# Other PSUM banks for four steps of a two-layer transformer kernel, and the last columns in quarters

## The chip, the core and the metric

The kernel runs on one core of a Trainium2 chip. The core has a matrix engine (TensorE, in the profile PE, with its weight loads shown apart as PEld), a vector engine (VectorE, DVE), a scalar engine (ScalarE, ACT), a general engine (GpSimd, POOL) and SyncE (SP), which here only issues transfers. Each engine runs its own instructions in order and waits on semaphores for the others. Data lies in SBUF; TensorE writes its sums into PSUM, which the kernel uses as eight banks of 128 partitions by 512 floats.

The metric is the device time of one launch in microseconds (us). Three runs of the kernel before took 711.92, 708.44 and 712.90 us, the median is 711.92. The profiled execution took 712.76 us; its span, from the first to the last instruction, is 711.0 us.

## The reference

Sixteen learned meta tokens stand ahead of 256 tokens of width 1024, so 272 columns pass through two layers. A layer is a mixer of three kinds of heads side by side, an output projection, and a feed-forward block with a squared ReLU:

```python
h = jnp.concatenate([meta, x], axis=1)                    # [1, 272, 1024]
for l in range(DEPTH):                                    # 2 layers
    u = rmsnorm(h, norm_mix[l])
    (qa, ka, va, qi, ki, wi, qb, kb, vb, qc, kc, vc, gc) = jnp.split(u @ w_in[l], split_pts, axis=-1)
    a_out = sparse_indexer_attention(qa, ka, va, qi, ki, wi, bias_a, topk=64)   # 8 heads of 64
    b_heads = diff_attention(qb, kb, vb, bias_b, lam)     # 4 heads: softmax - lam * softmax
    b_out = rmsnorm(b_heads, diff_norm[l]) * (1.0 - lambda_init)
    ret = retention(rotary(qc), rotary(kc), vc)           # 4 heads
    c_out = jax.nn.silu(gc) * rmsnorm(ret, ret_norm[l])
    h = h + jnp.concatenate([a_out, b_out, c_out], axis=-1) @ w_out[l]
    u = rmsnorm(h, norm_ff[l])
    h = h + jnp.square(jax.nn.relu(u @ w_ff1[l])) @ w_ff2[l]
return rmsnorm(h, final_norm)[:, N_META:]                 # [1, 256, 1024]
```

In the indexer the scores `relu(qi . ki)`, weighted by `wi`, choose the 64 keys that each query of the first kind of heads may see.

## The kernel before

**Units.** All weights are cut into 206 units of 1024 rows by 128 columns, 103 for each layer: 31 for the input projections, 8 for the output projection, 64 for the feed-forward block. The activations lie transposed, features on partitions and tokens on columns. A unit (function `slot`) is 24 matmuls: each of its eight 128x128 blocks is multiplied three times, since weights and activations are each split into a high part and a remainder (`hi`/`lo`, `uh`/`ul`): hi by uh (L189), hi by ul (L190), lo by uh (L191), all into one PSUM bank. SyncE loads the units ahead, ScalarE makes `hi` (L170), VectorE or, for some units, GpSimd makes `lo` (L182).

**Events.** Everything that is not a unit's matmul (scores, softmax, transposes, norms) is put between them by hand. `place(slot, p, f)` hangs the step `f` on slot `slot + p // 6` at one of six points: "evac" and "none" ahead of its matmuls, "quarter" after 6 of them, "half" after 12, "most" after 18, "all" after 24. The table `PLACES` holds the number `p` of each step, the table `AFTER` the distance of the steps that follow a unit. The order of the calls is the order on every engine, so an instruction that waits holds up everything behind it on its engine.

**Banks.** The eight banks are two rotating pools of four. `acc_bank()` takes the next bank of the units' pool (`mm` in the profile), `att()` the next of the other pool (`att`). A bank is given to a new holder in the order of the calls, and its first writer waits until the last reader of the holder four calls back is done.

**The steps that the change touches**, all in `mixer` and `ffn_rows`:

- `e_ki` (L462): the indexer's keys leave the first unit's bank. The product with the token factor goes once into `f` (`kf`, in SBUF) and once, rounded, into `kh`; the two L471 subtract `kh` from `f`, for the upper and the lower 64 partitions. `i_head` (L575) multiplies the keys by the queries.
- `b_values` (L766) calls `meta_v`: two transposes (L645) into an `att` bank, and a ScalarE copy to SBUF (L647), the values of the meta tokens for the differential heads. Pair 1 of these heads (`b_pair`, L726) takes two `att` and two `mm` banks; the exponentials (L599) go back into one of the `att` banks of each head, and `b_keys` (L747) reads it last.
- `r_pv` (L803): the value sums of the differential heads (w = 0) and of the retention heads (w = 1), into one bank `o` (L811, L817, L820); in layer 0 the meta tokens' sums go to a second bank `om` (L822). `r_norm` squares them, sums, and has GpSimd raise to the power -0.5 (L837); `r_scale` reads `o` last on VectorE (L844) and `om` (L849). `a_pair` (L662) takes two `att` banks for the scores of two heads of the first kind, `a_keys` (L605, copied by L606) one for the transposed weights.
- `ffn_rows`: in layer 1 the second feed-forward product is made by rows, tokens on partitions: for each of two blocks of 128 tokens (t) and two halves of 512 columns (a) one `att` bank `acc[t, a]` sums over 32 units (`pairs`, L1019). The last unit is done one half of the columns after the other. `last(t)` then makes `y` (L1048), its squares on ScalarE (L1049), `yg` (L1054), the sum of squares (L1056), the power on GpSimd (L1058), and the output in two halves (L1059 and L1061) with a transfer each on SyncE (L1060, L1062). After the last matmul only `last(1)` is left.

Of the kernel before, what the change touches and what calls it, by code (L numbers as in the profile page):

```python
# [8 lines left out]
F = mybir.dt.float32  # L9
R = mybir.dt.float32r  # L10
AF = mybir.ActivationFunctionType
# [35 lines left out]
    "a_pair": (105, 116, 134, 148),  # L47
    "a_norm": (109, 110, 119, 127, 137, 144, 155, 156),
    "a_keys": (117, 122, 127, 138, 145, 154, 163, 168),
    "b_values": (99,),  # L50
    "b_meta": (115,),
    "e_wi2": (28,),
    "r_pv": (124, 167),
# [47 lines left out]
def block_kernel(ctx: ExitStack, tc: tile.TileContext, W, hin, cst, onehot, rbe, par, fin, dlam, out):  # L101
# [337 lines left out]
    def mixer(l):  # L439
# [21 lines left out]

        def e_ki(ps):  # L462
            bc = bcast[key]
            f = ta("kf")
            k2 = ck([128, 2, T], R, "ki")
            kh, kl = k2[:, 0], k2[:, 1]
            V.tensor_tensor(f[64:128], ps[64:128, :T], bc[64:128], OP.mult)
            V.tensor_tensor(kh[64:128], ps[64:128, :T], bc[64:128], OP.mult)
            S.activation(kh[0:64], f[64:128], AF.Copy)
            for r in (slice(64, 128), slice(0, 64)):  # L470
                V.tensor_tensor(kl[r], f[64:128], kh[64:128].bitcast(F), OP.subtract)  # L471
            st["ki"] = kh, kl
# [327 lines left out]


        def r_pv(w):
            o = att()  # L803
            om = att() if first else None
            vball = st[("vb", "vc")[w]]
            x4 = st[("wT", "sT")[w]]
# [162 lines left out]
    def ffn_rows():  # L969
# [40 lines left out]
            S.activation(hi, r[:, q0:], AF.Copy)  # L1010
            V.tensor_tensor(lo, r[:, q0:], hi.bitcast(F), OP.subtract)

        def pairs(wt, k, t, which, halves=(0, 1)):

            xh, xl = (x[:, k % 4, 16 + 128 * t:144 + 128 * t] for x in sx[k // 4])
            w = [x.rearrange("p a c -> p (a c)") for x in wt]
            for x, part in {"hi": ((xh, 0), (xl, 0)), "lo": ((xh, 1),)}[which]:
                for a in halves:
                    PE.matmul(acc[t, a], x, w[part][:, 512 * a:512 * a + 512],  # L1019
                              start=k == 0 and x is xh and part == 0, stop=k == 31 and part == 1)  # L1020

        def second(i, k):
            fire(i, "evac")
# [15 lines left out]
            pairs((hi, lo), k, 1, "lo")  # L1039
            fire(i, "all")  # L1040

        ms = small.tile([128, 4], F, name="ms", bufs=1)

        def last(t):
            y = ck([128, 1024], F, "y")
            half = [slice(0, 512), slice(512, 1024)]
            for a, c in enumerate(half):
                V.scalar_tensor_tensor(y[:, c], acc[t, a], scale["r2"][:, t:t + 1], hT[t][:, c], OP.mult, OP.add)  # L1048
                S.activation(tb("junk", (128, 512)), y[:, c], AF.Square, scale=float(D) ** -0.5,  # L1049
                             accum_out=ms[:, 2 * t + a:2 * t + a + 1])  # L1050
            g = scale["g"]
            o = ck([128, 1024], F, "fo")
            yg = tb("yg", (128, 512))
            V.tensor_tensor(yg, y[:, half[0]], g[:, half[0]], OP.mult)  # L1054
            v = small.tile([128, 1], F, name="nv")
            V.scalar_tensor_tensor(v, ms[:, 2 * t:2 * t + 1], EPS, ms[:, 2 * t + 1:2 * t + 2], OP.add, OP.add)  # L1056
            r = small.tile([128, 1], F, name="nr")
            G.tensor_tensor(r, v, nhalf[:, :1], OP.pow)  # L1058
            S.activation(o[:, half[0]], yg, AF.Copy, scale=r)  # L1059
            nc.sync.dma_start(out[128 * t:128 * t + 128, half[0]], o[:, half[0]])  # L1060
            V.scalar_tensor_tensor(o[:, half[1]], y[:, half[1]], r, g[:, half[1]], OP.mult, OP.mult)  # L1061
            nc.sync.dma_start(out[128 * t:128 * t + 128, half[1]], o[:, half[1]])  # L1062

        at(b + 1, "half", factors)
        at(b + 1, "none", gains)
# [28 lines left out]
        for n in range(4):  # L1094
            if n == 1:
                last(0)
            for halves in ((0, 1),) if n < 3 else ((0,), (1,)):
                pairs(wt[n], 28 + n, 1, "hi", halves)
                pairs(wt[n], 28 + n, 1, "lo", halves)
        last(1)  # L1100

    def ffn(l):
# [152 lines left out]
```

## Time and profile before

| what | before |
|---|---|
| runs | 711.92, 708.44, 712.90 us (median 711.92) |
| profiled execution | 712.76 us, span 711.0 us |
| TensorE busy | 697.5 us (98%), 5244 matmuls |
| VectorE busy | 452.6 us (64%) |
| ScalarE busy | 388.4 us (55%) |
| GpSimd busy | 162.6 us (23%) |
| chain that ended last | 90% TensorE, 3% VectorE |

Busy is the time in which an engine has an instruction under way, so a matmul that runs at half the clock is busy for longer and does no more. The granted clock of TensorE is shown as a share of its full speed. A wait is idle time of an engine that ended when another engine's instruction signalled. A row of the timeline gives the start of an instruction in us from the start of the span, its duration, engine, line, operation, and output <- input with shapes; behind it in brackets stand the idle time before it and what ended that.

### The profile page before, as it was taken

The page shows a single profiled execution, that of the slowest core. Times are in us where ns is not written, and L with a number is a line of the kernel's source. Part 1 is how long each engine was busy: PE and PEld are TensorE (multiplying, and loading weights), DVE is VectorE, ACT ScalarE, POOL GpSimd, SP SyncE. Part 2 cuts the span into 40 slices and gives each one's busy share as a digit, 9 for nine tenths or more (in the row PEclk, how much of TensorE's full clock was granted, in tenths as well). Part 3 has the DMA queues.
Part 4 walks back from the last instruction along what each step waited for, and adds up shares of the span by engine and source line. Part 5 has one row for each costly group of instructions (what it writes and reads, how often), then busy time and mean ns, then how long its engine had stood idle before and what let it go on. Part 6 is the DMA issues. An engine that isn't in the chain of part 4 may idle for free.

```text
span 711.0 us, 13318 instructions
## 1 busy us (share of the span) xinstructions
PE 697.5 (98%) x5244; PEld 659.3 (93%) x5244; DVE 452.6 (64%) x893; ACT 388.4 (55%) x760; POOL 162.6 (23%) x140
## 2 busy tenths in 40 slices
PE   9998989999999999999999999999999999999996
PEld 8898989889999999999999999998999999999994
DVE  6689548648676666454545887595576555555554
ACT  7557656447465555444435668655565445454443
POOL 2657544023100000000004667540420000000000
PEclk9999989999999999999999999999999999999998
DMA  9686333234465545455554434333365556655521
GB/s 329 181 242 185 107 138 119 76 133 148 149 207 177 174 169 185 156 189 167 175 182 140 163 115 150 118 119 105 133 211 205 177 191 197 199 182 181 180 87 59
DMA packets 34610, 115.57 MB, mean 163 GB/s; under 512 B 4051, under 2 KB 6388, under 8 KB 34548
## 3 DMA queue, kind: packets, MB, share of 16 engines
q1 hardware_dynamic: 31392, 110.00, 46.3%
q10 hardware_dynamic: 3156, 4.72, 2.8%
q8 instruction: 41, 0.67, 0.4%
q14 instruction: 21, 0.17, 0.1%
HBM read 113.05 MB, written 1.66 MB: 161 GB/s over the span
## 4 chain that ended last, share of the span: by engine, by line
PE 90%; DVE 3%; issue 2%; ACT 1%; POOL 1%; DMA 1%; SPq 0%; POOLq 0%; ACTq 0%
PE mm L189 23%; PE mm L191 23%; PE mm L190 23%; PE att L1019 12%; PE att L662 1%; PE att L575 1%; PE att L605 1%; PE att L817 1%; DMA h<-hin 1%; PE att L705 1%; PE att L811 1%; PE att L820 1%; PE att L711 0%; PE att L784 0%; POOL hv L837 0%
## 5 line engine op out<-in xcount | busy, mean ns | idle before, releaser
L170 ACT ACTIVATE hi<-raw 128x1024 fp32r<-128x1024 f32 (+1 forms) x205 | 215.0, 1051 | 150.3 <-issue 74.6
L189 PE MATMUL mm<-uh,hi 128*128 128x272 f32 (+1 forms) x1008 | 297.0, 295 | 0.0
L191 PE MATMUL mm<-uh,lo 128*128 128x272 f32 (+1 forms) x1008 | 289.8, 287 | 0.3 <-DVE lo L182 0.3
L190 PE MATMUL mm<-ul,hi 128*128 128x272 f32 (+1 forms) x1008 | 288.6, 286 | 0.0
L182 DVE TENSOR_TENSOR lo<-raw,hi 128x1024 fp32r<-128x1024 f32 (+1 forms) x175 | 214.5, 1245 | 21.4 <-ACT hi L170 21.4
L189 PEld LDWEIGHTS mm<-uh,hi 128*128 128x128 f32 x1008 | 191.5, 190 | 8.1 <-issue 6.1
L190 PEld LDWEIGHTS mm<-ul,hi 128*128 128x128 f32 x1008 | 191.8, 190 | 1.3
L191 PEld LDWEIGHTS mm<-uh,lo 128*128 128x128 f32 x1008 | 191.2, 190 | 1.1 <-DVE lo L182 0.8
L182 POOL TENSOR_TENSOR lo<-raw,hi 128x1024 fp32r<-128x1024 f32 x34 | 82.1, 2424 | 51.0 <-ACT hi L170 50.9
L189 PE MATMUL mm<-sh,hi 128*128 128x272 f32 x256 | 74.2, 290 | 0.0
L191 PE MATMUL mm<-sh,lo 128*128 128x272 f32 x256 | 74.1, 289 | 0.0
L190 PE MATMUL mm<-sl,hi 128*128 128x272 f32 x256 | 73.7, 288 | 0.0
L298 POOL TENSOR_TENSOR sacc<-sacc,sq 128x272 f32<-128x272 f32 (+1 forms) x24 | 23.0, 958 | 209.9 <-ACT sq L296 209.5
L1002 DVE TENSOR_TENSOR fr<-fr 128x256 f32<-128x256 f32 x32 | 13.6, 426 | 58.4 <-ACT fr L1001 58.4
L190 PEld LDWEIGHTS mm<-sl,hi 128*128 128x128 f32 x256 | 48.3, 188 | 0.0
L189 PEld LDWEIGHTS mm<-sh,hi 128*128 128x128 f32 x256 | 48.2, 188 | 0.0
L191 PEld LDWEIGHTS mm<-sh,lo 128*128 128x128 f32 x256 | 48.2, 188 | 0.0
L1058 POOL TENSOR_TENSOR nr<-nv,cs 128x1 f32<-128x1 f32 x2 | 1.1, 560 | 179.6 <-DVE nv L1056 179.6
L1019 PE MATMUL att<-hi,sh 128*128 128x512 f32 x128 | 40.2, 394 | 0.0
L1019 PE MATMUL att<-hi,sl 128*128 128x512 f32 x128 | 40.1, 393 | 0.0
L189 PE MATMUL mm<-oh,hi 128*128 128x272 f32 (+1 forms) x128 | 37.0, 289 | 0.0
L190 PE MATMUL mm<-ol,hi 128*128 128x272 f32 (+1 forms) x128 | 36.6, 286 | 0.0
(232 smaller groups left out, 932.9 us busy)
## 6 DMA issues: line engine op xcount, KB each, us to landing
raw<-w SPq DMA_DIRECT2D x203, 512.0 KB, 3.5
h<-hin SPq DMA_DIRECT2D x4, 272.0 KB, 4.2
nb<-scr ACTq DMA_DIRECT2D x4, 272.0 KB, 4.5
raw<-w ACTq DMA_DIRECT2D x4, 256.0 KB, 4.9
out_dram<-fo SPq DMA_DIRECT2D x4, 256.0 KB, 2.0
cs<-cst ACTq DMA_DIRECT2D x1, 904.0 KB
scr<-row ACTq DMA_DIRECT2D x1, 600.0 KB
nb<-scr ACTq DMA_DIRECT2D x4, 136.0 KB, 5.1
```

Source lines behind the costliest of these rows:

```text
L170: S.activation(hi[:, p], raw[:, p], AF.Copy)
L182: eng.tensor_tensor(lo[:, p], raw[:, p], hi[:, p].bitcast(F), OP.subtract)
L189: PE.matmul(ps, hi[:, k, :], xh, start=first and j == 0, stop=False)
L190: PE.matmul(ps, hi[:, k, :], xl, start=False, stop=False)
L191: PE.matmul(ps, lo[:, k, :], xh, start=False, stop=last and j == len(ks) - 1)
L298: eng.tensor_tensor(sacc[part][:, q0:], sacc[part][:, q0:], sq[:, q0:], OP.add)
L575: PE.matmul(ps[:, sl], q[:, c:c + 128], k[:, :n], start=i == 0, stop=i == 1)
L605: PE.transpose(pt[:, a * 128:a * 128 + 128], p[:, c:c + 128], ident)
L662: PE.matmul(ps[:, sl], st["qa"][r, m, c:c + 128], st["ka"][r, m, 0:n], start=True, stop=True)
L705: PE.matmul(ps[:, q0:T], vb, st["pmT"][:, q0:], start=True, stop=False)
L1002: V.tensor_tensor(r[:, q0:], r[:, q0:], r[:, q0:], OP.mult)
L1019: PE.matmul(acc[t, a], x, w[part][:, 512 * a:512 * a + 512], start=k == 0 and x is xh and part == 0, stop=k == 31 and part == 1)
```

## The change

1. `b_values` is placed at 86 in place of 99: in slot 14 after 6 matmuls ("quarter"), where it was in slot 16 after 12 ("half"). It holds for both layers.
2. `e_ki` keeps the product `f` in an `att` bank of PSUM in place of SBUF.
3. `r_pv` takes the bank `o` from the units' pool; `om` stays in the other.
4. The last two units are done for the second token block first on columns 0 to 511, then 512 to 767, then 768 to 1023. `last(1)` reads the second half by these quarters; so there are three sums of squares and two small additions. The output of both blocks is written by quarters of 256 columns: ScalarE scales columns 0 to 255 and 256 to 511, VectorE 512 to 767 and 768 to 1023, and four transfers follow, three from SyncE and one from ScalarE's queue.

```diff
-    "b_values": (99,),
+    "b_values": (86,),
...
         def e_ki(ps):
             bc = bcast[key]
-            f = ta("kf")
+            f = att()[:, :T]
...
         def r_pv(w):
-            o = att()
+            o = acc_bank()
             om = att() if first else None
...
-        def pairs(wt, k, t, which, halves=(0, 1)):
+        def pairs(wt, k, t, which, cols=(slice(0, 512), slice(512, 1024))):
...
-                for a in halves:
-                    PE.matmul(acc[t, a], x, w[part][:, 512 * a:512 * a + 512],
-                              start=k == 0 and x is xh and part == 0, stop=k == 31 and part == 1)
+                for c in cols:
+                    a, b = divmod(c.start, 512)
+                    PE.matmul(acc[t, a][:, b:b + c.stop - c.start], x, w[part][:, c],
+                              start=k == 0 and x is xh and part == 0, stop=k == 31 and part == 1 and c.stop % 512 == 0)
...
-            for a, c in enumerate(half):
-                V.scalar_tensor_tensor(y[:, c], acc[t, a], scale["r2"][:, t:t + 1], hT[t][:, c], OP.mult, OP.add)
-                S.activation(tb("junk", (128, 512)), y[:, c], AF.Square, scale=float(D) ** -0.5,
+            for a, c in enumerate([slice(0, 512), slice(512, 768), slice(768, 1024)] if t else half):
+                b, n = c.start % 512, c.stop - c.start
+                V.scalar_tensor_tensor(y[:, c], acc[t, c.start // 512][:, b:b + n], scale["r2"][:, t:t + 1],
+                                       hT[t][:, c], OP.mult, OP.add)
+                S.activation(tb("junk", (128, 512))[:, :n], y[:, c], AF.Square, scale=float(D) ** -0.5,
                              accum_out=ms[:, 2 * t + a:2 * t + a + 1])
...
-            V.scalar_tensor_tensor(v, ms[:, 2 * t:2 * t + 1], EPS, ms[:, 2 * t + 1:2 * t + 2], OP.add, OP.add)
+            if t:
+                V.scalar_tensor_tensor(ms[:, 2:3], ms[:, 2:3], EPS, ms[:, 3:4], OP.add, OP.add)
+                V.tensor_tensor(v, ms[:, 2:3], ms[:, 4:5], OP.add)
+            else:
+                V.scalar_tensor_tensor(v, ms[:, 0:1], EPS, ms[:, 1:2], OP.add, OP.add)
             r = small.tile([128, 1], F, name="nr")
             G.tensor_tensor(r, v, nhalf[:, :1], OP.pow)
-            S.activation(o[:, half[0]], yg, AF.Copy, scale=r)
-            nc.sync.dma_start(out[128 * t:128 * t + 128, half[0]], o[:, half[0]])
-            V.scalar_tensor_tensor(o[:, half[1]], y[:, half[1]], r, g[:, half[1]], OP.mult, OP.mult)
-            nc.sync.dma_start(out[128 * t:128 * t + 128, half[1]], o[:, half[1]])
+            for a in range(2):
+                c, d = slice(256 * a, 256 * a + 256), slice(512 + 256 * a, 768 + 256 * a)
+                S.activation(o[:, c], yg[:, c], AF.Copy, scale=r)
+                V.scalar_tensor_tensor(o[:, d], y[:, d], r, g[:, d], OP.mult, OP.mult)
+                (nc.scalar if a else nc.sync).dma_start(out[128 * t:128 * t + 128, c], o[:, c])
+                nc.sync.dma_start(out[128 * t:128 * t + 128, d], o[:, d])
...
+        for c in (slice(0, 512), slice(512, 768), slice(768, 1024)):
+            for n in (2, 3):
+                pairs(wt[n], 28 + n, 1, "hi", [c])
+                pairs(wt[n], 28 + n, 1, "lo", [c])
         last(1)
```

How TensorE's and VectorE's rows stand is shown at three places. A row names the line, the operation, output <- input with the tiles' numbers, and the semaphores that it waits for, by engine.

On TensorE in layer 0, before the change, the scores of pair 1 (L726) follow the units' rows, and the two transposes of `b_values` come some 50 rows behind them, inside a unit; `att` and `mm` are banks of the two pools, `kb` and `qb` keys and queries, `vbdT` the meta values.

```order
L726 MATMUL att_941<-kb_474,qb_585 128x144 [waits DVE_49]
L726 MATMUL mm_942<-kb_474,qb_585 128x144
L726 MATMUL att_943<-kb_474,qb_585 128x144 [waits Activation_49]
L726 MATMUL mm_944<-kb_474,qb_585 128x144 [waits DVE_49]
...
L191 MATMUL mm_1056<-uh_81,lo_936 128x272
L645 MATMUL att_1082<-cs_84,vbdT_121 128x128 [waits DVE_49]
L645 MATMUL att_1082<-cs_84,vbdT_121 128x128
L189 MATMUL mm_1056<-uh_81,hi_886 128x272
```

After the change, at the same place:

```order
L191 MATMUL mm_915<-uh_81,lo_834 128x272
L645 MATMUL att_922<-cs_84,vbdT_121 128x128 [waits DVE_49]
L645 MATMUL att_922<-cs_84,vbdT_121 128x128
L189 MATMUL mm_915<-uh_81,hi_740 128x272
...
L726 MATMUL att_946<-kb_474,qb_585 128x144 [waits Activation_49]
L726 MATMUL mm_947<-kb_474,qb_585 128x144
L726 MATMUL att_948<-kb_474,qb_585 128x144 [waits DVE_49]
```

The transposes now stand six unit matmuls ahead of pair 1, and the pair's two `att` banks are each one further on in the rotation: its third bank waits for VectorE where it waited for ScalarE.

The second place is the third pair of scores of the first kind of heads (`a_pair(2)`), behind the value sums of layer 0, on TensorE; `ka` and `qa` are its keys and queries. Before:

```order
L191 MATMUL mm_1421<-uh_81,lo_1300 128x272
L662 MATMUL att_1428<-ka_801,qa_1054 128x144 [waits Activation_49]
L662 MATMUL att_1429<-ka_801,qa_1054 128x144 [waits DVE_49]
L662 MATMUL att_1428<-ka_801,qa_1054 128x272
L662 MATMUL att_1429<-ka_801,qa_1054 128x272
```

After:

```order
L191 MATMUL mm_1421<-uh_81,lo_1300 128x272
L662 MATMUL att_1428<-ka_801,qa_1059 128x144
L662 MATMUL att_1429<-ka_801,qa_1059 128x144 [waits Activation_49]
L662 MATMUL att_1428<-ka_801,qa_1059 128x272
L662 MATMUL att_1429<-ka_801,qa_1059 128x272
```

The second bank waited for VectorE (L844, which reads the value sums); now it waits for ScalarE. The value sums themselves (L811 to L820) stand in the same rows as before, with `mm` in place of `att`.

The third place is the end of VectorE's program, `last(1)`; `y`, `yg`, `nv` and `fo` are the tiles of the final norm, a row with x2 stands for two. Before:

```order
L1048 SCALAR_TENSOR_TENSOR y<-att,r_6596,hT 128x512 [waits PE_49] x2
L1054 TENSOR_TENSOR yg<-y,fg 128x512 [waits DVE_49]
L1056 SCALAR_TENSOR_TENSOR nv<-ms 128x1 [waits Activation_49]
L1061 SCALAR_TENSOR_TENSOR fo<-y,nr,fg 128x512 [waits Pool_49]
```

After:

```order
L1050 SCALAR_TENSOR_TENSOR y<-att,r_6596,hT 128x512 [waits PE_49]
L1050 SCALAR_TENSOR_TENSOR y<-att,r_6596,hT 128x256 [waits PE_49]
L1050 SCALAR_TENSOR_TENSOR y<-att,r_6596,hT 128x256
L1057 TENSOR_TENSOR yg<-y,fg 128x512 [waits DVE_49]
L1060 SCALAR_TENSOR_TENSOR ms<-ms 128x1 [waits Activation_49]
L1061 TENSOR_TENSOR nv<-ms 128x1 [waits DVE_49,Activation_49]
L1069 SCALAR_TENSOR_TENSOR fo<-y,nr,fg 128x256 [waits Pool_49]
L1069 SCALAR_TENSOR_TENSOR fo<-y,nr,fg 128x256
```

The second half's `y` is two rows, of which the first carries the wait for TensorE and the second none; there is one more small sum, and the last product is two rows.

## Rows read from the trace of the kernel before

**Rows 1.** Waits of TensorE: instruction <- engine waited for: us, times, longest.

```profile
PE att L645 <- DVE bp L747: 2.3, 1, 2.3
PE att L662 <- DVE on L844: 2.0, 1, 2.0
...
PE att L575 <- DVE ki L471: 0.7, 1, 0.7
```

**Rows 2.** Table by stretches: length, PE, PEld, DVE, ACT, POOL busy, clock, DMA share, GB/s.

```profile
18.00:69.00 51.00, 50.26 (x407) 47.36 (x405) 42.03 (x151) 31.11 (x76) 33.41 (x22) 1.00 0.74 200
71.40:75.20 3.80, 3.79 (x18) 3.79 (x19) 3.65 (x10) 1.68 (x4) 3.57 (x5) 0.55 0.34 98
...
102.70:109.20 6.50, 6.50 (x28) 5.79 (x29) 5.22 (x18) 3.81 (x12) 5.39 (x6) 0.51 0.23 74
109.20:704.00 594.80, 594.65 (x4479) 562.83 (x4476) 374.50 (x653) 318.36 (x588) 102.45 (x86) 1.00 0.47 157
```

**Rows 3.** Timeline of TensorE, matmuls of units at 105 and at 109 us.

```profile
105.19 0.43 PE L189 MATMUL mm<-uh,hi 128*128 128x272 f32 x1
105.42 0.43 PE L190 MATMUL mm<-ul,hi 128*128 128x272 f32 x1
...
109.30 0.37 PE L189 MATMUL mm<-uh,hi 128*128 128x272 f32 x1
...
109.77 0.29 PE L189 MATMUL mm<-uh,hi 128*128 128x272 f32 x1
109.89 0.28 PE L190 MATMUL mm<-ul,hi 128*128 128x272 f32 x1
```

**Rows 4.** Timeline of VectorE, TensorE and ScalarE around pair 1, 56 to 73 us.

```profile
55.94 0.27 DVE L621 TENSOR_TENSOR mt<-att,nb 16x128 f32<-16x128 f32 x1
...
60.34 0.76 DVE L747 SCALAR_TENSOR_TENSOR bp<-att,bsm,bp 128x144 f32<-128x144 f32 x2
...
61.01 0.39 PE L726 MATMUL att<-kb,qb 32*128 32x144 f32 x1
...
70.39 0.97 DVE L747 SCALAR_TENSOR_TENSOR bp<-att,bsm,bp 128x144 f32<-128x144 f32 x2 [0.59 <-POOL bp L742]
...
72.48 0.37 ACT L647 ACTIVATE vm<-att 128x256 f32<-128x256 f32 x1
```

**Rows 5.** Timeline of VectorE and ScalarE around the wait at L662.

```profile
98.36 0.18 DVE L456 TENSOR_TENSOR vbdT<-mm,bf 128x32 f32<-128x32 f32 x1
...
99.56 0.47 ACT L606 ACTIVATE pT<-att 128x384 f32<-128x384 f32 x1
...
101.92 0.69 DVE L844 TENSOR_TENSOR on<-att,hv 128x512 f32<-128x512 f32 x1 [2.19 <-POOL hv L837]
...
104.09 0.31 DVE L596 CUSTOM_DVE_ANT_0 ap<-att,ap 128x144 f32<-128x144 f32 x1 [1.16 <-PE att L662]
```

**Rows 6.** Groups of VectorE by line and form: busy us, mean ns of one, idle before.

```profile
L471 DVE TENSOR_TENSOR ki<-kf,ki 64x272 fp32r<-64x272 f32 x4 | 4.5, 1123 | 0.1
L494 DVE TENSOR_TENSOR qi<-mm,qi 64x256 fp32r<-64x256 f32 x16 | 6.8, 422 | 10.6 <-ACT qi L493 10.6
...
25.23 2.60 DVE L471 TENSOR_TENSOR ki<-kf,ki 64x272 fp32r<-64x272 f32 x2
```

**Rows 7.** Timeline of all engines at the end of the program.

```profile
703.42 1.43 DVE L1048 SCALAR_TENSOR_TENSOR y<-att,r,hT 128x512 f32<-128x512 f32 x2 [1.32 <-PE att L1019]
703.68 0.39 PE L1019 MATMUL att<-lo,sh 128*128 128x512 f32 x1
704.77 0.68 DVE L1054 TENSOR_TENSOR yg<-y,fg 128x512 f32<-128x512 f32 x1
...
705.88 0.56 POOL L1058 TENSOR_TENSOR nr<-nv,cs 128x1 f32<-128x1 f32 x1 [4.56 <-DVE nv L1056]
```

**Rows 8.** Timeline of ScalarE and TensorE, two transposes of weights and the copy between.

```profile
109.36 0.49 ACT L606 ACTIVATE pT<-att 128x384 f32<-128x384 f32 x1 [0.31 <-PE att L605]
...
113.52 0.49 PE L605 MATMUL att<-cs,ap 128*128 128x128 f32 x3
```

More of the change, by code (lines that the diff above doesn't have):

```diff
@@ L1040, in second @@
             fire(i, "all")
-        ms = small.tile([128, 4], F, name="ms", bufs=1)
+        ms = small.tile([128, 6], F, name="ms", bufs=1)
         def last(t):
@@ L1096, in ffn_rows @@
                 last(0)
-            for halves in ((0, 1),) if n < 3 else ((0,), (1,)):
-                pairs(wt[n], 28 + n, 1, "hi", halves)
-                pairs(wt[n], 28 + n, 1, "lo", halves)
+            if n < 2:
+                pairs(wt[n], 28 + n, 1, "hi")
+                pairs(wt[n], 28 + n, 1, "lo")
+        for c in (slice(0, 512), slice(512, 768), slice(768, 1024)):
+            for n in (2, 3):
+                pairs(wt[n], 28 + n, 1, "hi", [c])
+                pairs(wt[n], 28 + n, 1, "lo", [c])
         last(1)
```

## The prediction

> **What bounds the kernel now.** I read the page first. TensorE is busy for nearly the whole span, and the chain that ended last is mostly its matmuls, so whatever shortens the program must shorten TensorE's row, or what follows its last matmul. The second view is the list of waits, kept to TensorE [rows 1]. It is short: 2.3 us at L645, the transposes of the first differential values; 2.0 us at L662, a pair of attention scores; 0.7 us at L575, the indexer's scores. The other two are shorter than L575's or lie ahead of the first weights. All three named lie in layer 0; layer 1 has the same waits written into it and none shows.
>
> The third view is the table by stretches, with the clock that TensorE was granted [rows 2]. From 18 to 69 us it is 1.00 (2.4 GHz, the upper of its two levels). From 71.4 to 75.2, just behind the 2.3 us of idling, the mean is 0.55, and from 102.7 to 109.2, just behind the 2.0 us, 0.51; from 109.2 to 704 it is 1.00 again. The lower level, 0.50, is 1.2 GHz, so by these means it held for (1 - 0.55) x 2 x 3.8 = 3.4 us and (1 - 0.51) x 2 x 6.5 = 6.4 us. The timeline shows what it costs [rows 3]: the same 272-column matmul starts 0.12 us after the one before it at full clock (109.89 after 109.77), 0.23 us at half (105.42 after 105.19). A stretch at half clock therefore loses 1 - 0.12/0.23 = 0.48 of its length by the matmuls' own starts, and less where other work than matmuls sets the pace; taking 0.44 to 0.5, that is 1.5 to 1.7 us in the first stretch and 2.8 to 3.2 us in the second.
>
> The Trainium skill (TensorE: Matmul & The Clock Gate, What's actually happening) says that the default is throttled, that activity releases it, and that a gate steered by how busy TensorE has been decides it. The trace agrees: both falls stand right behind the only two idle times of 2 us or more after the start.
>
> **The change part by part.**
>
> *First differential values earlier.* Two transposes and one ScalarE copy move from slot 16 to slot 14. Their bank at L645 was the one in which the scores of pair 1 were still held for head 2; VectorE's L747 released it, running from 70.39 to 71.36 [rows 4]. At the new place, six unit matmuls ahead of pair 1, which began at 61.01, the bank is that of the meta rows' scores, read by L621 until 56.2, some 4 us earlier, so the 2.33 us go, and with them the 1.5 to 1.7 us of clock: I take 1.6. The transposes themselves cost TensorE the same at either place. The copy, 0.37 us [rows 4], joins ScalarE ahead of a weight copy; ScalarE is busy 31.1 of the 51 us from 18 to 69 [rows 2], so its idle time hides the copy, and without that cover it would cost at most its 0.37 us. What is late next is pair 1 itself, two rows on in TensorE's order: its third bank is now head 0's, which L747 releases at 60.34 + 0.76 = 61.10, while TensorE began the pair at 61.01 [rows 4] and now reaches the third bank about 0.2 us later, behind the pair's first two scores. Margin 0.1 us; if VectorE does not move up with TensorE's 0.7 us from below, the wait is 0.6 us.
>
> *Value sums in the units' banks.* L811 to L820 fill a bank that L844 reads last. It was an `att` bank, and L662 wanted it: VectorE had waited 2.19 us for GpSimd's power (L837) when L844 began, L844 ran until 102.61, and TensorE idled 2.01 us [rows 1, 5]. Now an `mm` bank is held instead, and the pair's second bank comes from L606's copy, which ended at 100.03 [rows 5]. The 2.01 us go, and with them 2.8 to 3.2 us of clock: I take 3.0. The new holder leaves three banks to the units. The unit that now follows this bank's older holder started at 109.30 [rows 3], and that holder's reader, L456, ended at 98.54 [rows 5]: 10.8 us, and still over 5 when the 2.0 and 3.0 us won above are taken off.
>
> *`kf` in PSUM.* In layer 0 L471 subtracts two SBUF tiles in 2.60 us for its two instructions, while GpSimd subtracts weights; the mean of L471 is 1123 ns, that of L494, the same shape nearly with one input in PSUM, 422 ns, over 16 of them [rows 6]. With `kf` in PSUM I take L494's price: 0.9 us for both. L471 also has to wait for ScalarE's read of the same bank, 0.1 us. The 0.71 us at L575 goes; bounds 0 and 0.7 us.
>
> The Trainium skill (SBUF — State Buffer, Who interferes with whom) says that a VectorE instruction with two SBUF inputs contends with a GpSimd instruction that reads SBUF, and one with a single SBUF input does not. The trace agrees, as far as L471 against L494 goes.
>
> *The end.* The order on TensorE after the change finishes the first half of the columns 12 quarter matmuls before its end, so `y` for it is out of the way; the 24 quarter matmuls cost what 12 halves did, by the 0.12 us from one 272-column matmul to the next [rows 3] and 703.68 + 0.39 for the last half [rows 7]. But in VectorE's order the first quarter's row carries a wait on TensorE and the second quarter's carries none: the first already waits for the bank's last matmul. Nothing of the second half starts before TensorE ends. Before: last matmul until 704.07, GpSimd's power at 705.88, 1.81 us [rows 7]. After: two quarters of `y`, half of L1048's pair of 1.43 us, so 0.7 us; the product `yg`, 0.68 us; that ends where it ended before, at 705.45 in the old time, and 0.43 us went from there to the power, for one small sum that waited a little for ScalarE's squares. Now there are two small sums and no such wait: 0.4 to 0.5 us, 1.8 to 1.9 in all. No gain. Behind the power the copies are half as long, so the first transfer starts sooner, but SyncE issues three where it issued two, and what ends last is its last. Bounds for the end: gained, the start of one quarter and half a copy, 0.4 us by half of one of L1048's two rows; lost, 0.2 us by the second small sum and one more issue, from the same rows' remainders; I take 0.
>
> The Trainium skill (PSUM — Partial Sum Buffer, PSUM bank collisions raise a hardware error) has the rule that speaks against this part: guard PSUM by bank, not by address, since two engines on one bank collide even at disjoint columns. By it the quarter split wins nothing over the halves; by its absence it would win the start of one quarter, some 0.4 us.
>
> *New waits.* TensorE arrives earlier at everything later, so other margins shrink. At L605 for head 4 (113.52) the reader of its bank, L606, ended at 109.36 + 0.49 = 109.85 [rows 8], a margin of 3.7 us, of which the 5.0 us won above are taken. The softmax ahead of that reader moves up too, but by little: its first row, L596 at 104.09, stands behind only 1.16 us of VectorE's idling [rows 5], and what VectorE did before is not moved. That leaves a wait of 5.0 - 3.7 - 1.0, about 0.3 us, and 1.3 us if the softmax does not move at all. With pair 1's 0 to 0.6 I put down 0.8 us in all, bounds 0 and 2.0.
>
> **The sum.** 2.33 + 1.6 + 2.01 + 3.0 + 0.71 - 0.8 = 8.85 us. The profiled execution took 712.76 us (span 711.0, 1.7 outside it): 703.9 us. The profiled time lies 0.84 above the median of the three runs; the spread of those runs, over 4 us, is as large as these clock stretches, which the changed kernel should not have. I predict 703.6 us.
>
> **The rivals.**
> (A) As summed: 703.6, own range 701.0 to 706.0. Chance 0.68.
> (B) The waits go but low clock remains, or a new wait is long enough to bring it back. For: a margin of 0.1 us at pair 1 and a negative one at L605. Against: 0.7 us of idling at L575 left the clock at 1.00. Gain 5.05 - 0.8 us, and up to half of the 4.6: 706 to 708.5. Chance 0.20.
> (C) The change doesn't do it: the stall only moves, from L645 to pair 1 or from L662 to the next row that takes an `att` bank: VectorE still waits its 2.19 us for L837, and L844 still ends at 102.6. One of the two pairs of terms stays, and the other's gain is partly eaten: 708.5 to 713. Chance 0.08.
> (D) Slower. The value sums hold an `mm` bank until L844, in both layers, and a unit waits for a bank. For: three banks where there were four, and a holder that itself waits for GpSimd. Against: the margin of over 5 us worked out above. It decides from a lag that grows by 9 to 10 us: the gain of 8.85 is then gone. Waits of 5 us with 3 us of clock behind them, in each of the two layers, add 16 to 703.9: 719 to 722. Chance 0.04.
>
> **Numbers.** About 1% is what a measurement of this kernel tells from no change: 704.8 and below is faster. A lies there in 0.85 of its cases, B in 0.05: faster 0.59, slower 0.04, same 0.37. The range 701.0 to 709.0 holds A nearly whole and most of B.
>
> **What would show it.** Right: no wait at L645 and L662 in the list of waits, L575 under 0.1 us, the granted clock at 1.00 from 18 us to the end of the matmuls, L471 near 440 ns, L605 with under 1 us. The distance from the last matmul to the power of the last token block stays at 1.8 to 1.9 us; the first quarter's L1050 starts at TensorE's end. Wrong: any stretch at half clock after 18 us, or an idle time of over 1.5 us at L726 or L605.

## The result, and the profile after

The changed kernel took 703.77 us (median of six runs, 703.40 to 704.39), the kernel before 711.37 in six runs beside them (708.44 to 712.90). The medians lie 7.6 us apart, the means 7.1 (710.96 and 703.82): the kernel before spreads over more than 4 us, the changed one over 1. The ratio of the means is 0.990, with a 95% interval of 0.9879 to 0.992: faster by 1.0%. Forecast were 703.6 us and 701.0 to 709.0. The profiled execution took 703.40 us, its span 701.6 us against 711.0, so 9.4 us are to be found in the trace; the sum had 8.85.

The waits of TensorE after the change (instruction <- engine waited for: us in total, times, longest) answer [rows 1]:

```profile
PE att L253 <- POOL z L250: 1.0, 1, 1.0
PE mm L191 <- DVE lo L182: 0.6, 1, 0.6
PE att L605 <- ACT pT L606: 0.6, 1, 0.6
PE mm L189 <- ACT uh L289: 0.4, 1, 0.4
```

L645, L662 and L575 are gone. L605 with 0.6 us is new. The rest lies in the first 8 us, where the weights come in.

The table by stretches after the change answers [rows 2]. Its columns are the length, the busy time of PE, PEld, DVE, ACT and POOL with the number of instructions, the granted clock, the busy share of the DMA engines, GB/s:

```profile
18.00:69.00 51.00, 51.00 (x417) 48.52 (x416) 41.28 (x154) 32.32 (x77) 33.45 (x22) 1.00 0.74 201
69.00:102.00 33.00, 32.97 (x268) 30.38 (x266) 19.42 (x59) 21.47 (x61) 19.55 (x20) 1.00 0.42 140
102.00:110.00 8.00, 7.40 (x56) 6.47 (x56) 7.79 (x17) 5.57 (x13) 6.72 (x9) 1.00 0.45 145
110.00:694.00 584.00, 583.83 (x4401) 553.42 (x4401) 365.02 (x641) 313.74 (x579) 99.26 (x78) 1.00 0.48 158
```

The clock is 1.00 from 18 us to the end of the matmuls, in the stretch with the 0.6 us of idling too (102 to 110). To see where the time went, the same instruction is looked up in both timelines, here on TensorE after the change:

```profile
63.58 0.49 PE L605 MATMUL att<-cs,bp 128*128 128x128 f32 x3
...
90.83 0.49 PE L605 MATMUL att<-cs,ap 128*128 128x128 f32 x3
...
98.51 0.49 PE L605 MATMUL att<-cs,ap 128*128 128x128 f32 x3
...
103.96 0.55 PE L605 MATMUL att<-cs,ap 128*128 128x128 f32 x3 [0.60 <-ACT pT L606]
...
694.59 0.28 PE L1020 MATMUL att<-lo,sh 128*128 128x256 f32 x1
```

The same in the kernel before:

```profile
64.48 0.49 PE L605 MATMUL att<-cs,bp 128*128 128x128 f32 x3
...
95.75 0.49 PE L605 MATMUL att<-cs,ap 128*128 128x128 f32 x3
...
108.59 0.73 PE L605 MATMUL att<-cs,ap 128*128 128x128 f32 x3
```

The fourth started at 113.52 [rows 8], the last matmul at 703.68 [rows 7]; it ended at 704.07 and ends now at 694.87. The lead of the changed kernel grows like this:

| up to | lead | grew by | forecast | what lies in it |
|---|---|---|---|---|
| L605 of the first differential head | 0.90 | 0.90 | 0.71 | `kf` in PSUM |
| L605 ahead of the third pair of L662 | 4.92 | 4.02 | 2.33 + 1.6 | transposes of `b_values` earlier, first stretch at half clock gone |
| L605 at 98.51 | 10.08 | 5.16 | 2.01 + 3.0 | value sums in an `mm` bank, second stretch gone |
| L605 at 103.96 | 9.56 | -0.52 | -0.8 | the new wait |
| end of the last matmul | 9.20 | -0.36 | none | pieces of 0.1 to 0.3 us, spread over 590 us |
| end of the span | 9.4 | +0.2 | 0 | the end |

The two transposes of `b_values` stand in the first of these stretches after the change and in the second before it. They cost about 0.25 us (L190 starts at 59.57 behind them, where it would have at about 59.34), and just ahead of them the lead is 0.95. Without them the first row is 0.95 and the second 3.97.

### The profile page after: what moved, and what is told of

It is laid out like the page before. It is cut to its first block, busy times and chain, and to the rows that moved or that the text cites. A ratio compares the mean times of both kernels' runs of the same rounds, so it can differ in the third digit from the quotient of the medians.

```text
span 701.6 us, 13354 instructions
## 1 busy us (share of the span) xinstructions
PE 692.0 (99%) x5250; PEld 654.5 (93%) x5250; DVE 448.1 (64%) x897; ACT 388.5 (55%) x764; POOL 165.0 (24%) x140
## 4 chain that ended last, share of the span: by engine, by line
PE 95%; ACT 1%; issue 1%; DVE 1%; DMA 1%; POOL 0%; POOLq 0%; SPq 0%; ACTq 0%; DVEq 0%
PE mm L189 25%; PE mm L191 24%; PE mm L190 24%; PE att L1020 12%; PE att L605 1%; PE att L575 1%; PE att L662 1%; PE mm L817 1%; PE att L705 1%; PE mm L811 1%; DMA pr<-par 1%; PE mm L820 1%; PE att L711 0%; PE att L726 0%; PE att L784 0%
## 5 line engine op out<-in xcount | busy, mean ns | idle before, releaser
L190 PE MATMUL mm<-ul,hi 128*128 128x272 f32 (+1 forms) x1008 | 287.4, 285 | 0.1
L182 DVE TENSOR_TENSOR lo<-raw,hi 128x1024 fp32r<-128x1024 f32 (+1 forms) x175 | 212.3, 1232 | 21.5 <-ACT hi L170 21.4
L190 PEld LDWEIGHTS mm<-ul,hi 128*128 128x128 f32 x1008 | 190.1, 189 | 1.6 <-DVE ul L290 0.3
L182 POOL TENSOR_TENSOR lo<-raw,hi 128x1024 fp32r<-128x1024 f32 x34 | 83.0, 2447 | 49.2 <-ACT hi L170 49.2
L190 PE MATMUL mm<-sl,hi 128*128 128x272 f32 x256 | 73.7, 288 | 0.0
L190 PEld LDWEIGHTS mm<-sl,hi 128*128 128x128 f32 x256 | 48.3, 188 | 0.0
L1020 PE MATMUL att<-hi,sh 128*128 128x512 f32 (+1 forms) x130 | 40.7, 391 | 0.0
L1020 PE MATMUL att<-hi,sl 128*128 128x512 f32 (+1 forms) x130 | 40.6, 390 | 0.0
L190 PE MATMUL mm<-ol,hi 128*128 128x272 f32 (+1 forms) x128 | 36.6, 286 | 0.0
```

What stands on the lines that cost most here:

```text
L182: eng.tensor_tensor(lo[:, p], raw[:, p], hi[:, p].bitcast(F), OP.subtract)
L190: PE.matmul(ps, hi[:, k, :], xl, start=False, stop=False)
L1020: PE.matmul(acc[t, a][:, b:b + c.stop - c.start], x, w[part][:, c], start=k == 0 and x is xh and part == 0, stop=k == 31 and part == 1 and ...
```

## The experiments

The times below are medians of 4 to 8 runs of each kernel. The kernel before, run beside them, had 711.39, 711.54 and 711.14 us in the three groups, and the changed kernel 703.34 and 703.73 in the two groups in which it ran again, so that absolute times can be set side by side to about 0.4 us.

A finer measure comes from the traces. The executions differ by up to 1.2 us in their first 27 us, in which the first weights come in. The time from the start of TensorE's first L575 row to the end of its last matmul leaves that out, and leaves out what follows the last matmul:

```profile
26.95 0.23 PE L575 MATMUL att<-ki,qi 128*128 128x144 f32 x1
27.89 0.63 PE L575 MATMUL att<-ki,qi 128*128 128x144 f32 x3 [0.71 <-DVE ki L471]
```

This is the kernel before; in the changed kernel the four matmuls follow each other:

```profile
26.93 0.63 PE L575 MATMUL att<-ki,qi 128*128 128x144 f32 x4
```

| kernel | first L575 | end of the last matmul | between |
|---|---|---|---|
| before | 26.95 | 704.07 | 677.12 |
| changed, three traces | 26.93, 26.95, 27.60 | 694.87, 694.81, 695.46 | 667.94, 667.86, 667.86 |
| `b_values` put back | 27.14 | 698.94 | 671.80 |
| value sums put back | 26.89 | 697.92 | 671.03 |
| `kf` put back | 26.79 | 695.61 | 668.82 |
| waits filled | 27.21 | 699.98 | 672.77 |
| three edits, old end, two traces | 26.83, 28.01 | 694.62, 695.81 | 667.79, 667.80 |
| three edits, only the output in quarters | 26.97 | 694.77 | 667.80 |
| quarters in banks of their own | 27.34 | 695.23 | 667.89 |
| the same, `a_keys` later | 27.80 | 695.69 | 667.89 |

The other versions are described below. Traces of one program agree here to 0.1 us.

### One edit put back at a time

`b_values` again at 99:

```diff
-    "b_values": (86,),
+    "b_values": (99,),
```

> The changed kernel with `b_values` put back to 99. Theory (each edit carries its own wait and the half-clock stretch behind it): the wait at L645 is back with 2.3 us, the granted clock falls to 0.5 for about 3.4 us behind it, and the time is 703.8 + 2.3 + 1.6 = 707.7 us. Rival 1 (the low clock costs nothing of its own, or comes from somewhere else): 703.8 + 2.3 = 706.1 us, or the clock stays at 1.00. Rival 2 (this edit was not needed, since the other edits move the banks too): 703.8 us, no wait at L645.

Measured: 707.24 us (707.22 to 707.50), 3.5 more than the 703.77 of the changed kernel, and 3.9 by the table (671.80 against 667.9). The wait is back with its 2.33 us, and the clock falls behind it:

```profile
70.67 0.44 PE L645 MATMUL att<-cs,vbdT 128*128 128x128 f32 x2 [2.33 <-DVE bp L747]
```

```profile
69.00:72.00 3.00, 1.33 (x8) 1.33 (x9) 2.27 (x7) 1.97 (x5) 2.54 (x5) 0.89 0.55 178
72.00:76.00 4.00, 4.00 (x24) 3.85 (x23) 3.76 (x7) 1.06 (x4) 4.00 (x5) 0.66 0.41 133
76.00:80.00 4.00, 4.00 (x33) 3.64 (x34) 1.95 (x11) 3.42 (x12) 4.00 (x5) 1.00 0.39 131
```

By the clock column the low level held for 0.11 x 2 x 3 + 0.34 x 2 x 4 = 3.4 us, as long as in the kernel before. Rival 1 (706.1) and rival 2 (703.8) fall.

The bank of the value sums again from `att()`:

```diff
-            o = acc_bank()
+            o = att()
```

> The changed kernel with the value sums' bank `o` put back to `att()`. Theory: the wait at L662 is back with 2.0 us, the low clock behind it with 3.0 to 3.2, and the new wait of 0.6 us at L605 goes: 703.8 + 5.1 - 0.6 = 708.3 us. Rival 1 (low clock costs nothing of its own): 703.8 + 2.0 - 0.6 = 705.2 us. Rival 2 (the wait is absorbed, since TensorE comes to L662 at another time): under 704.5 us.

Measured: 706.56 us (706.46 to 706.91), 2.8 more than the changed kernel, between the theory and rival 1. The wait at L662 is back with 2.0 us, and the wait at L605 is gone; behind 18 us TensorE's list of waits has this line alone:

```profile
PE att L662 <- DVE on L844: 2.0, 1, 2.0
```

The clock tells the rest:

```profile
95.00:98.00 3.00, 1.00 (x6) 0.64 (x7) 1.01 (x2) 1.49 (x4) 3.00 (x3) 0.94 0.53 175
98.00:101.00 3.00, 3.00 (x13) 2.30 (x12) 1.89 (x10) 1.56 (x7) 3.00 (x4) 0.50 0.00 0
101.00:104.00 3.00, 3.00 (x26) 3.00 (x25) 2.89 (x8) 2.21 (x7) 1.89 (x3) 0.99 0.41 141
```

The low level held for 0.4 + 3.0 + 0.1 = 3.4 us here, against 6.4 in the profiled execution of the kernel before [rows 2], behind a wait of the same length. At 0.48 of its length it costs 1.6 us, and 2.0 + 1.6 - 0.6 = 3.0 us; measured are 2.8, and 3.1 by the table. So the edit is worth 2.0 us of idling plus a clock term that is not the same in each execution.

`kf` again in SBUF:

```diff
-            f = att()[:, :T]
+            f = ta("kf")
```

> The changed kernel with `kf` put back to SBUF. Theory: L471 takes 1.3 us again in layer 0, L575 waits 0.7 us for it, clock untouched: 703.8 + 0.7 to 0.9 = 704.5 to 704.7 us. Rival (the gain at L575 is eaten by a later wait, at pair 1, in the changed kernel): no difference, 703.8 us.

Measured: 704.23 us (704.18 to 704.41), 0.5 to 0.9 more than the changed kernel's three medians of 703.34 to 703.77, with the wait back in the list:

```profile
PE att L575 <- DVE ki L471: 0.7, 1, 0.7
```

The median lies between the theory's 704.5 and the rival's 703.8 and doesn't decide by itself. The table does: 668.82 against 667.9, so 0.9 us are lost up to the last matmul, and the gain isn't eaten later. The groups of VectorE by line in the changed kernel answer [rows 6]:

```profile
L471 DVE TENSOR_TENSOR ki<-att,ki 64x272 fp32r<-64x272 f32 x4 | 1.8, 445 | 0.2
```

L471 takes 445 ns in place of 1123. What made the difference can be read in the kernel before, where one L471 of each pair stands beside a weight subtraction of GpSimd (L182) and the other behind it. The first line is GpSimd's, the second gives the shortest, median and longest of the four L471 in ns:

```profile
24.69 2.39 POOL L182 TENSOR_TENSOR lo<-raw,hi 128x1024 fp32r<-128x1024 f32 x1
```

```profile
L471 DVE TENSOR_TENSOR ki<-kf,ki x4: 436/954/2150, 25.2 to 389.1; 64x272 fp32r<-64x272 f32 x4
```

In layer 0 the first L471, the longest, runs from 25.23 to 27.38, until 0.3 us behind the end of GpSimd's instruction at 27.08. The second has two SBUF inputs as well, but GpSimd is idle beside it: 0.44 us. In layer 1 it is 1.47 us beside GpSimd and 0.44 behind it. In the changed kernel GpSimd's subtraction stands at the same place (24.67 to 27.07), and both L471, with one input in PSUM, take 0.445 us. So neither the two SBUF inputs nor GpSimd's work make it slow alone, but both together. That agrees with what the Trainium skill (SBUF — State Buffer, Who interferes with whom) says of instructions of VectorE with two SBUF inputs.

### The waits filled with matmuls

The kernel before, in layer 0 with 20 matmuls ahead of L645 and 18 ahead of the third pair of L662, into a bank that nobody reads:

```diff
+        def fill(n):
+            ps = acc_bank()
+            for j in range(n):
+                PE.matmul(ps[:, :T], uh[:, j % 8, 16:144], uh[:, (j + 1) % 8, :], start=True, stop=True)
```

> The kernel before with 20 unit-sized matmuls ahead of L645 (2.5 us, into a bank of the units' pool that nobody reads) and 18 ahead of the third pair of L662 (2.25 us): they lie in the two waits, which remain. Theory (the low clock is the follow-up of the idling and costs by itself): the clock stays at 1.00 and the time is the profiled 712.8 less 1.6 and 3.0, plus 0.4 by which the matmuls outlast the waits: 708.6 us, with a spread of under 1 us. Rival (the low clock costs nothing, or is not tied to the idling): 711.5 to 712 us.

Measured: 708.67 us (708.42 to 709.08; the kernel before, beside it, 711.54, 709.14 to 712.97). TensorE does work that nobody wants in place of idling, and the kernel is faster by 2.9 us. Against the profiled execution of the kernel before, which the forecast took as its base, it is 677.12 - 672.77 = 4.35 us by the table, where 4.2 were forecast. The table by stretches:

```profile
69.00:72.00 3.00, 3.00 (x26) 2.96 (x25) 2.24 (x9) 1.96 (x5) 1.90 (x5) 1.00 0.66 234
72.00:78.00 6.00, 6.00 (x50) 5.49 (x49) 5.85 (x17) 3.52 (x9) 5.78 (x8) 1.00 0.29 104
...
98.00:103.00 5.00, 5.00 (x39) 4.49 (x38) 2.20 (x8) 2.60 (x8) 5.00 (x6) 1.00 0.30 105
103.00:110.00 7.00, 7.00 (x56) 6.61 (x55) 6.76 (x19) 5.79 (x17) 5.78 (x6) 1.00 0.42 135
```

The clock stays at 1.00 through both places. So the low clock follows from the idling, and it costs by itself. The spread of the kernel before goes with it: its 37 runs lie between 708.44 and 713.16 us. Of the 31 whose mean granted clock was taken, the four with 0.990 are the longest (712.8 to 713.2 us), and those with 0.996 or more lie at 708.8 to 710.7. Without the two stretches the spread is 0.7 us.

### The end

The kernel before with the three bank edits alone, its old matmuls, `last` and two transfers kept:

```diff
-    "b_values": (99,),
+    "b_values": (86,),
...
-            f = ta("kf")
+            f = att()[:, :T]
...
-            o = att()
+            o = acc_bank()
```

> The kernel before with the three bank edits and its old end (halves, two transfers). Theory (the quarters win nothing): 703.8 us, between 703.5 and 704.0; the power of the last block 1.8 us behind the last matmul. Rival (the quarters carry part of the gain): 704.2 us or more.

Measured: 704.95 us (704.23 to 705.24), 1.2 us more than the changed kernel. The theory that the end is worth nothing falls. Up to the last matmul the two agree (667.79 and 667.9 in the table), so the difference lies behind it. Its trace, at the end:

```profile
696.44 0.56 POOL L1058 TENSOR_TENSOR nr<-nv,cs 128x1 f32<-128x1 f32 x1 [4.57 <-DVE nv L1056]
...
697.78 0.33 SPq L1060 DMA_DIRECT2D out_dram<-fo  x1
698.22 0.38 SPq L1062 DMA_DIRECT2D out_dram<-fo  x1
```

and the changed kernel's:

```profile
694.90 0.87 DVE L1050 SCALAR_TENSOR_TENSOR y<-att,r,hT 128x256 f32<-128x256 f32 x2 [0.68 <-PE att L1020]
...
695.70 0.68 DVE L1057 TENSOR_TENSOR yg<-y,fg 128x512 f32<-128x512 f32 x1
...
696.30 0.15 DVE L1060 SCALAR_TENSOR_TENSOR ms<-ms 128x1 f32<-128x1 f32 x1
696.55 0.16 DVE L1061 TENSOR_TENSOR nv<-ms 128x1 f32<-128x1 f32 x1
696.79 0.57 POOL L1065 TENSOR_TENSOR nr<-nv,cs 128x1 f32<-128x1 f32 x1 [4.73 <-DVE nv L1061]
...
697.93 0.33 SPq L1070 DMA_DIRECT2D out_dram<-fo  x1
698.33 0.39 ACTq L1070 DMA_DIRECT2D out_dram<-fo  x1
698.35 0.92 SPq L1071 DMA_DIRECT2D out_dram<-fo  x2
```

Up to the power the changed kernel is as forecast: `y` starts at TensorE's end, and the power comes 696.79 - 694.87 = 1.92 us behind it (1.81 before, 1.8 to 1.9 forecast). From the power's start to the end of the span, however, it takes 701.6 - 696.79 = 4.8 us, the kernel before 711.0 - 705.88 = 5.1 us, and the three edits with the old end 702.4 - 696.44 = 6.0 us. The DMA in short stretches at the end of the latter shows what is late (the last two columns are the busy share of the 16 DMA engines and GB/s):

```profile
699.50:700.00 0.50, 0.00 (x0) 0.00 (x0) 0.00 (x0) 0.00 (x0) 0.00 (x0) 0.50 0.94 361
700.00:700.50 0.50, 0.00 (x0) 0.00 (x0) 0.00 (x0) 0.00 (x0) 0.00 (x0) 0.50 0.08 12
700.50:701.00 0.50, 0.00 (x0) 0.00 (x0) 0.00 (x0) 0.00 (x0) 0.00 (x0) 0.50 0.04 16
```

About one of 16 DMA engines works on for 0.85 us after the others are done. The trace's packet records have a single 8 KB packet of an instruction queue (q14 on the page) at 699.6 us, among the output's. In the kernel before, the same queue's last 8 KB packet comes at 711.7 us, behind the output, and its tail is 5.1 us with the same code.

Three runs followed. First the same two kernels again, on one chip:

> The changed kernel again, as the measure for the runs beside it: 703.8 us, between 703.4 and 704.4.

Measured: 703.34 us (703.18 to 704.44).

> The three bank edits with the old end, again, beside the changed kernel on the same chip. Theory 1 (the end wins nothing, and the 704.95 us seen before was that chip's): the same as the changed kernel within 0.2 us. Theory 2 (the old end is slower behind its last transfer's issue: 4.2 us to the span's end in that trace, against 2.8 in the changed kernel's): 0.8 to 1.3 us more than the changed kernel.

Measured: 704.85 us (704.58 to 705.44): theory 2. The tail behind the power is 6.0 us again (703.6 - 697.63). The profiled execution also lost 0.9 us at the bias table's matmul at the start (L395, waiting for a transfer); it is the longest of its five runs. By the traces alone, from the last matmul to the end of the span, the old end is 1.82 + 6.0 = 7.8 us and the new one 1.92 + 4.8 = 6.7, a difference of 1.1 us of the 1.5 between the medians.

Then the output alone by quarters, with matmuls, `y` and sums by halves:

```diff
+            for a in range(2):
+                c, d = slice(256 * a, 256 * a + 256), slice(512 + 256 * a, 768 + 256 * a)
+                S.activation(o[:, c], yg[:, c], AF.Copy, scale=r)
+                V.scalar_tensor_tensor(o[:, d], y[:, d], r, g[:, d], OP.mult, OP.mult)
+                (nc.scalar if a else nc.sync).dma_start(out[128 * t:128 * t + 128, c], o[:, c])
+                nc.sync.dma_start(out[128 * t:128 * t + 128, d], o[:, d])
```

> The three bank edits, the old matmuls and the old `y` by halves, and only the output written by quarters in four transfers. If the smaller transfers carry the gain of the end: as the changed kernel or 0.1 to 0.3 us less, since the small sums are not split. If the quarter matmuls and `y` by quarters carry it: as the three edits with the old end.

Measured: 703.23 us (703.10 to 704.23), the same as the changed kernel. So what the end wins, it wins by the output in quarters: its tail behind the power is 701.4 - 696.59 = 4.8 us. The matmuls and `y` by quarters win nothing, as forecast. That is also what the prediction drew from the rule of the Trainium skill on PSUM banks (PSUM — Partial Sum Buffer, PSUM bank collisions raise a hardware error); in the trace the first quarter's `y` starts at 694.90, at the last matmul's end, and whether the shared bank is the reason isn't shown by this run.

Last, whether the late 8 KB packet is moved by SyncE's count of instructions, with three more transfers ahead of the end:

```diff
-            nc.sync.dma_start(g, bass.AP(tensor=fin.tensor, offset=fin.offset, ap=[[0, 128], [1, D]]))
+            for a in range(4):
+                nc.sync.dma_start(g[:, 256 * a:256 * a + 256],
+                                  bass.AP(tensor=fin.tensor, offset=fin.offset + 256 * a, ap=[[0, 128], [1, 256]]))
```

> The three bank edits with the old end, and the load of the final gains split in four, so that SyncE issues three transfers more, some 190 us ahead of the end. In the two traces of the old end with the three edits a single 8 KB transfer of the instruction queue falls among the last output packets: one DMA engine of 16 is still busy from 700 to 700.9 us when the others are done, and the end comes 0.85 us later than in the kernel before. Theory (that transfer brings SyncE's next instructions and falls there by the count of SyncE's instructions): with three issues more it comes earlier, the tail behind the power is 5.1 to 5.2 us in place of 5.96, and the time 0.8 us lower than the 704.85 of the three edits: 704.0 us. Rival (two large transfers land late by themselves): 704.8 us, tail 5.9.

Measured: 704.34 us (704.09 to 704.62), beside 703.73 for the changed kernel. The packet did not move: it starts at 699.7 us, and one DMA engine is late by 0.85 us again; the tail is 702.3 - 696.49 = 5.8 us. The theory on SyncE falls. Which engine's program that packet belongs to, and so what moves it, stays open; in the changed kernel and the one with the output alone by quarters it came at 687 us. That it makes the old end late is read from three traces that have it there and two (the kernel before, and the one with the filled waits, whose tail is 5.2 us) that have it behind the output; no run moved it alone.

The nine traces with the output in quarters narrow it down. In eight of them the packet comes at 687 to 692 us; in the one with `kf` put back it comes at 698.6, just ahead of the first output transfer, issued at 698.67. The tail is 4.8 us in all nine. So of the 1.2 us between the tails some 0.3 are the smaller transfers' own (4.8 against the 5.1 to 5.2 of the old end with the packet behind it), and the rest goes with the packet's place. No trace has the quarters with the packet among them, so whether they would be late too, and whether they are what moved it, isn't shown.

### Two tries to go further

> The changed kernel once more, as the measure for the three runs beside it: 703.4 us, between 703.2 and 704.4.

Measured: 703.73 us (703.32 to 704.04).

The last quarters in banks of their own, `yg` ahead of them:

```diff
+        early.append(ck([128, 1024], F, "y"))
+        V.scalar_tensor_tensor(early[0][:, 512:], acc[1, 1], scale["r2"][:, 1:2], hT[1][:, 512:], OP.mult, OP.add)
+        for a, c in enumerate((slice(0, 512), slice(512, 768), slice(768, 1024))):
+            if a:
+                tail[a] = acc_bank()
...
+                if a == 1 and t:
+                    yg = tb("yg", (128, 512))
+                    V.tensor_tensor(yg, y[:, half[0]], scale["g"][:, half[0]], OP.mult)
```

> The changed kernel, with the last two units' sums for columns 512 to 767 and 768 to 1023 in a bank of their own each (from the units' pool), the rest of that half added to hT ahead of time, and yg ahead of the quarters. Theory (in the changed kernel the first quarter's y waits for the last matmul only because both quarters lie in one bank): the first quarter's y starts 0.7 us before the last matmul ends, the power comes 1.5 us behind the last matmul in place of 1.92, and the time is 0.4 us lower than the changed kernel: 703.0 us. Rival (VectorE waits for the last matmul for another reason): the distance stays at 1.9 us.

Measured: 703.60 us (703.08 to 703.80), not to be told from the changed kernel. VectorE at its end:

```profile
694.69 0.69 DVE L1055 TENSOR_TENSOR yg<-y,fg 128x512 f32<-128x512 f32 x1
...
695.30 0.87 DVE L1057 SCALAR_TENSOR_TENSOR y<-mm,r,y 128x256 f32<-128x256 f32 x2
...
696.99 0.56 POOL L1073 TENSOR_TENSOR nr<-nv,cs 128x1 f32<-128x1 f32 x1 [4.57 <-DVE nv L1069]
```

The last matmul ends at 694.95 + 0.28 = 695.23. The first quarter's `y` now waits for nothing, but `yg` ahead of it, which was moved there, keeps VectorE until 695.38. So the run doesn't decide whether the shared bank alone held it back: it met neither the 1.5 us of the theory nor the 1.9 of the rival. The power comes 1.76 us behind the last matmul in place of 1.92.

The same, with `a_keys` of head 4 one place later:

```diff
-    "a_keys": (117, 122, 127, 138, 145, 154, 163, 168),
+    "a_keys": (117, 122, 127, 138, 146, 154, 163, 168),
```

> As the run before it, and a_keys of head 4 placed at 146 in place of 145, six unit matmuls later. Theory (the 0.6 us wait at L605 is only a bank that comes 0.6 us late): the wait goes and 0.5 to 0.6 us with it: 702.4 to 702.6 us. Rival (the wait moves to the pair of scores behind it): as the run before it, 703.0 us.

Measured: 703.70 us (703.32 to 704.07). The waits of TensorE:

```profile
PE att L395 <- DMA rb<-rbe: 1.2, 1, 1.2
...
PE att L662 <- DVE ol L868: 0.3, 1, 0.3
```

The 0.6 us at L605 are gone and 0.3 of them stand at the next pair of scores. This profiled execution lost 1.2 us at L395 at its start, a wait that the executions of other versions show with 0.9, 0.4 or nothing, and that hides gains of this size in the times. The table leaves it out and decides for the rival: 667.89 with the placement and 667.89 without, so nothing of the 0.6 us was won. Neither version beats the changed kernel by what can be measured.

## Why the prediction was right, point by point

**The sum.** Against the profiled execution the sum had 8.85 us, and the trace 9.2 up to the last matmul and 9.4 in all. The 703.6 stated is 0.3 under the 703.9 that the sum gives; that step is a judgement from the spread of the runs and has no term.

**The bound.** TensorE's row was the program, and the three waits named were its only large gaps. Their removal showed in full at the end: 9.56 us of lead at 104 us, 9.20 at the last matmul.

**First differential values.** 3.93 us forecast; 3.97 in the trace, when the transposes' own time is left out; put back, 3.9 by the table and 3.5 by the medians. Pair 1 (L726), named as late next, did not wait.

**Value sums.** 5.01 forecast, 5.16 in the trace. Put back, the edit cost 2.8 by the medians and 3.1 by the table, because 0.6 us of new waiting go with it and the low clock then held 3.4 us, not 6.4. The term of 3.0 us for the clock was the profiled execution's, which is among the longest of the kernel before; in the run that put the edit back it was 1.6. The prediction took the profiled time as its base and so the two fit together; against the median of before, 711.37, the gain is 7.6 us.

**`kf`.** 0.71 forecast, 0.95 at the first row behind the indexer's first head, 0.9 by the table when put back: 0.2 over the upper bound of 0.7. The listed wait counts from the end of the matmul before it; the next matmul started 0.94 us after that one's start and starts 0.13 after it now, 0.8 us, and the rest isn't explained. L471 takes 445 ns, about 440 were forecast, and the cause named, GpSimd beside two SBUF inputs, is the one that the trace shows.

**New waits.** 0.8 us forecast, in two places; 0.6 came, at L605 for head 4, the one worked out there as 0.3 to 1.3. It left the clock at 1.00.

**The end.** Taken at 0, with 0.4 gained to 0.2 lost as bounds. Against the kernel before it was 0.2 us, inside. As an edit of its own it was mis-sized: with the three bank edits in place, leaving it out costs 1.2 and 1.5 us by the medians (0.6 with three more transfers on SyncE), 1.1 by the traces, since the two large transfers then end 0.85 us late. The step that failed is "Behind the power ... what ends last is its last": it counted issues and bytes and had no term for another packet on the output's DMA engines. That the 0 fits against the kernel before is luck: there the packet came behind the output. That the quarters of the matmuls win nothing held; the prediction counts 24 of them for 12 halves, the trace has 12 for 6 (5250 matmuls against 5244), which changes nothing in it.

**The rivals.** B had the low clock remain; no stretch of it is left. C and D did not come: no bank of the units' pool is waited for. The margin of 5 us for D was enough, and by how much was not tried.

## What to carry to other kernels

Look behind every idle time of TensorE of some length for the granted clock: here waits of 2.0 and 2.3 us cost 3.4 to 5.2 us each, idling and slow stretch together, and matmuls that nobody wants, put into the two waits, won back 2.9 of the 7.6 us alone. With rotating banks ask who reads the bank last, four calls back; a step with a slow last reader belongs into the pool whose next turn is furthest away. Make the sum against the profiled execution's own time, and see whether that execution is typical before the result is set against a median. Where executions differ at their start, compare the time between two rows that all versions have: here it told 0.1 us apart, where the medians told 0.4.

## What the runs showed of the hardware that was not expected

The lower clock level held for 3.4 us behind one wait of 2.0 us and for 6.4 us behind another of the same length at the same place. One 8 KB packet of an instruction queue among the output's last packets kept one DMA engine of 16 busy 0.85 us longer than the others, and with it the end of the kernel, in each of the three traces that have it there. VectorE's subtraction with two SBUF inputs took 2.15 us beside GpSimd's and 0.44 behind it; with one input in PSUM it took 0.445 beside GpSimd's.
